# Earlier small loads and longer distances between VectorE pieces and the TensorE work that follows them, in a one-core DiT block

## The chip, the cores and the metric

The kernel runs on one core of a Trainium2 chip. Its metric is the device time in microseconds, the median of three runs. Five engines work beside each other, each through its own instructions in order: TensorE (PE, matmuls; PEld is its weight load), VectorE (DVE), ScalarE (ACT), GpSimd (POOL) and SyncE (SP), which here only issues DMAs. All of the large loads go out on SP.

## The reference

One block over 512 latent tokens and 256 context tokens of width 2048, in float32:

```python
mod   = silu(c) @ w_mod + b_mod            # 6 vectors of 2048; mod_c likewise from c_ctx
h_lat = rms_norm(x, nw[0]) * (1 + sc_m) + sh_m        # h_ctx likewise, with mod_c
p     = concat(h_ctx, h_lat) @ w_in
# lru: centred 4-tap conv of p's first 1024 columns, gates by 128x128 blocks, scans forward
#      and backward over context and latents; times gelu of the next 1024 columns
# gdn: conv + silu of q, k, v (8 heads of 128), l2-normalized q and k, beta and decay g from 32
#      gate columns, chunked delta rule forward and backward; rms_norm, times silu(z)
x = x + g_m * rms_norm(concat(lru, gdn)[latents] @ w_out, nw[1])
h = rms_norm(x, nw[2]) * (1 + sc_f) + sh_f
x = x + g_f * rms_norm(square(relu(h @ w_ff1)) @ w_ff2, nw[3])
```

The delta rule is, for each head and direction, a triangular solve within a chunk and a chain of state steps from chunk to chunk. Only the latents are returned.

## The kernel before

**Float32 by three products.** A weight piece is split into a rounded part `wh` (cast on ScalarE, L67) and a residue `wl` (subtraction on VectorE or GpSimd, L61), each with 3 buffers of 128x512, and each product of weights and activations is three matmuls: high by high, low by high, high by low. In the rows of the profile these are triples of lines: L338/341/342 (modulation), L524/525/526 (w_in), L1418/1419/1420 (w_out), L1467-1469, L1497-1499 and L1508-1510 (feed-forward).

**The stages.** (i) To about 135 us: c and c_ctx (16 rows of 128 each) and b_mod are loaded as rows of one page `pg`, turned into columns by a TensorE transpose against `ident` (function `columns`, L152; the copy behind it is L153), then `silc` = silu(c) and `csn`, its copy in matmul form (L171), are made on VectorE. 32 pieces of w_mod (tile `mr`, 1 MB each, 8 buffers; function `mload`, on SP) are split and multiplied. The context rows are normalized beside it. The small parameters (norm_w, the lru and gdn vectors) are loaded as rows of two more pages, `v2` and `v3`, and turned by `columns` behind the third piece (`if j == 2`). Two others, gdn_a_log and gdn_dt_bias, go into `alog`. (ii) To about 1085 us: the products with w_in, and beside them everything between the projections. (iii) To about 1480 us: the products with w_out (`project`, L1418-1420). (iv) The feed-forward to the end.

**Stage (ii) is the one that matters here.** `run_tiles` goes through a string of letters, `ORD`, one letter a column tile: k and l the gate columns of context and latents, c and g the q, k and v columns of the context's and the latents' heads, u and x the lru's input, y and z the two gates. A latent tile streams 512 columns, a context tile 256. A tile is four quads of 12 matmuls, the "streamed" matmuls; between quads the other work is put in. That work is a set of Python generators, and each `yield v, a, wait` ends a piece of it:

```python
                    if n == LAT or q % 2:
                        slot()
                        boundary()
```

`slot()` stands behind each quad of a latent tile and each second quad of a context tile. It gives a budget of 2.8 us of VectorE and 2.2 us of ScalarE (`RATE_V`, `RATE_A`) and lets tasks take their next piece while both budgets are positive; v and a are the piece's estimated costs in us, and `wait` is the number of slots that the task then sits out. All waits are written as multiples of H0, H1, H2 or H3, and all four are 1. Evacuations of tiles come first, then the tasks by priority. `boundary()` adds ordering edges, so that an instruction can't be moved more than 3 slots ahead on TensorE, SP and GpSimd, 2 on ScalarE and 1 on VectorE. So a piece that ends with a VectorE instruction and goes on with a TensorE one puts the TensorE instruction `wait` slots behind in TensorE's stream, and TensorE, which goes through its instructions in order, stops there if VectorE hasn't come that far.

**The pieces that the change touches.** In `gates` (L694, L715): the copy of the gate tile, its transposes, the softplus and the beta on VectorE (L693 among it), the cumulative sums on TensorE (L697 is the matmul that starts them). In `normed2` (L755): l2-normalized tokens on VectorE, then their transposes on TensorE (`transp`, L255). In `Group.evac` (L807): silu as tanh on ScalarE and a product on VectorE (helper line L64), then transposes (L255 again). In `Group.run`, for a group of heads (two context groups of four heads, four latent groups of two): the inversion of the triangular blocks, 31 elimination steps on VectorE (L927 is a transpose at their end), then copies of the blocks (L937-940), then products of pairs of 32x32 blocks on TensorE (L951) and of 64x64 blocks (L981/982), then state steps (L1024, L1038, L1048), then the outputs' rescaling (L1090) and their transposes (L255).

In `project`, a product over a pair of heads whose rows are not there yet runs `slot()` and `boundary()` until they are.

## Time and profile before

| | |
|---|---|
| median of 3 runs | 2808.57 us (2805.38 to 2812.1) |
| the profiled execution, its own time | 2803.51 us |
| its span | 2801.70 us |
| TensorE's granted clock, mean | 0.979 |
| TensorE, VectorE, ScalarE, GpSimd busy | 95, 60, 42, 21% of the span |
| bytes moved by DMA | 434.33 MB, mean 155 GB/s |

How to read it: "busy" leaves out waiting and the issuing of DMAs. In a row of groups or waits, the part before "<-" is what an instruction writes, behind it what it reads, with buffer numbers left out; in a row of waits the form is waiting instruction <- what it waited for, then total us, times, longest. In the timeline a row is start, duration, engine, line, operation, tiles, shapes and in brackets the wait just before it. "Granted clock" is the share of full speed that the chip's throttle gave TensorE. In the windows, each engine's busy time in a stretch stands with its count of instructions.

### The profile page before, as it was taken

The numbers are of one execution on the slowest core, as the hardware profiler recorded it, in microseconds if no ns is written. First come the engines' busy times: TensorE is split into PE (matmuls) and PEld (weight loads), VectorE is DVE, ScalarE is ACT, GpSimd is POOL, SyncE is SP. The second block draws the span as 40 slices with busy tenths as digits, with TensorE's granted clock in tenths as the row PEclk, the third lists the DMA queues.
The fourth block names the chain that finished last, engine by engine and source line by source line (L and its number), as shares of the span: only waits on it lengthen the run. The fifth ranks groups of instructions, "written<-read, shape, count | busy, mean of one in ns | idle before, by whom it ended". The sixth has DMA issues, their size and how long they took to land.

```text
span 2801.7 us, 39553 instructions
## 1 busy us (share of the span) xinstructions
PE 2654.4 (95%) x14253; PEld 2178.3 (78%) x14253; DVE 1682.8 (60%) x3287; ACT 1187.9 (42%) x2418; POOL 586.1 (21%) x552
## 2 busy tenths in 40 slices
PE   6989899899999998988999999999999999999998
PEld 2378797788777887776898887888888888888886
DVE  5786767777696777847598433444433444334436
ACT  4556576654556564535552222222222222222223
POOL 1155354344244354326310000000000000000002
PEclk9999999999999999989999999999999999999999
DMA  9664465566566667646778333333333333333335
GB/s 331 215 177 126 109 187 166 153 187 190 168 189 189 200 198 222 212 150 212 235 258 277 119 98 113 98 98 98 98 98 98 94 96 97 98 98 98 98 98 154
DMA packets 374968, 434.33 MB, mean 155 GB/s; under 512 B 22665, under 2 KB 212450, under 8 KB 374770
## 3 DMA queue, kind: packets, MB, share of 16 engines
q1 hardware_dynamic: 373984, 431.59, 49.6%
q8 instruction: 112, 1.84, 0.3%
q14 instruction: 86, 0.70, 0.1%
q10 hardware_dynamic: 786, 0.19, 0.0%
HBM read 401.31 MB, written 30.41 MB: 154 GB/s over the span
## 4 chain that ended last, share of the span: by engine, by line
PE 57%; DVE 4%; DMA 2%; POOL 1%; issue 1%; ACT 1%; SPq 0%; DVEq 0%; ACTq 0%; POOLq 0%
PE bk L1510 8%; PE bk L1508 8%; PE bk L1509 8%; PE bk L1497 7%; PE bk L1498 7%; PE bk L1499 7%; PE bk L1420 2%; PE bk L1419 2%; PE bk L1418 2%; PE bk L1469 1%; DVE pg L61 1%; PE bk L1468 1%; PE bk L1467 1%; DVE wl L61 1%; PE bk L524 1%
## 5 line engine op out<-in xcount | busy, mean ns | idle before, releaser
L67 ACT CAST wh<-wr 128x512 fp32r<-128x512 f32 x952 | 584.6, 618 | 1217.1 <-PE bk L1498 443.9
L61 DVE TENSOR_TENSOR wl<-wr,wh 128x512 fp32r<-128x512 f32 x642 | 464.1, 725 | 761.6 <-ACT wh L67 643.3
L61 POOL TENSOR_TENSOR wl<-wr,wh 128x512 fp32r<-128x512 f32 (+1 forms) x310 | 402.4, 1304 | 609.9 <-ACT wh L67 555.1
L1510 PE MATMUL bk<-wl,pg 128*128 128x512 f32 x960 | 373.6, 389 | 0.9 <-DVE wl L61 0.9
L1509 PE MATMUL bk<-wh,pg 128*128 128x512 f32 x960 | 373.5, 389 | 0.0
L1508 PE MATMUL bk<-wh,pg 128*128 128x512 f32 x960 | 373.5, 389 | 0.0
L1497 PE MATMUL bk<-H2h,wh 128*128 128x512 f32 x896 | 349.9, 390 | 0.0
L1499 PE MATMUL bk<-H2h,wl 128*128 128x512 f32 x896 | 349.0, 390 | 0.0
L1498 PE MATMUL bk<-H2l,wh 128*128 128x512 f32 x896 | 349.0, 390 | 0.0
L524 PE MATMUL bk<-Hlh,wh 128*128 128x512 f32 (+1 forms) x784 | 316.5, 404 | 0.0
L526 PE MATMUL bk<-Hlh,wl 128*128 128x512 f32 (+1 forms) x784 | 309.9, 395 | 1.8 <-POOL wl L61 1.8
L525 PE MATMUL bk<-Hll,wh 128*128 128x512 f32 (+1 forms) x784 | 310.1, 396 | 0.0
L61 POOL TENSOR_TENSOR big<-big,pg 128x512 f32<-128x512 f32 x9 | 12.0, 1340 | 1247.5 <-ACT pg L1570 1247.5
L1510 PEld LDWEIGHTS bk<-wl,pg 128*128 128x128 f32 x960 | 180.2, 188 | 38.8 <-DVE wl L61 1.3
L1508 PEld LDWEIGHTS bk<-wh,pg 128*128 128x128 f32 x960 | 180.2, 188 | 37.3
L1509 PEld LDWEIGHTS bk<-wh,pg 128*128 128x128 f32 x960 | 180.2, 188 | 37.2
L1498 PEld LDWEIGHTS bk<-H2l,wh 128*128 128x128 f32 x896 | 168.5, 188 | 35.4 <-issue 0.5
L1497 PEld LDWEIGHTS bk<-H2h,wh 128*128 128x128 f32 x896 | 168.6, 188 | 35.3 <-issue 0.2
L1499 PEld LDWEIGHTS bk<-H2h,wl 128*128 128x128 f32 x896 | 168.5, 188 | 35.2
L526 PEld LDWEIGHTS bk<-Hlh,wl 128*128 128x128 f32 (+1 forms) x784 | 148.4, 189 | 35.8 <-POOL wl L61 2.3
L524 PEld LDWEIGHTS bk<-Hlh,wh 128*128 128x128 f32 (+1 forms) x784 | 149.1, 190 | 30.9 <-ACT pg L1071 0.2
L525 PEld LDWEIGHTS bk<-Hll,wh 128*128 128x128 f32 (+1 forms) x784 | 148.8, 190 | 29.9
(346 smaller groups left out, 4514.5 us busy)
## 6 DMA issues: line engine op xcount, KB each, us to landing
wr<-in_w_ff SPq DMA_DIRECT2D x272, 512.0 KB
wr<-in_w_in SPq DMA_DIRECT2D x144, 512.0 KB
ld<-in_w_mod SPq DMA_DIRECT2D x256, 256.0 KB
mr<-in_w_mod SPq DMA_DIRECT2D x32, 1024.0 KB
wr<-in_w_out SPq DMA_DIRECT2D x64, 512.0 KB
pg<-vkD SPq DMA_DIRECT2D x88, 128.0 KB
ld<-in_x SPq DMA_DIRECT2D x32, 256.0 KB
vkD<-pg SPq DMA_DIRECT2D x24, 256.0 KB
```

The lines of the kernel that those rows point to most:

```text
L61: e.tensor_tensor(out=out, in0=a, in1=b, op=op)
L67: S.copy(hi, src)
L524: T.matmul(pt[:m, :n], wh, a, start=k == 0, stop=False)
L525: T.matmul(pt[:m, :n], wh, b, start=False, stop=False)
L526: T.matmul(pt[:m, :n], wl, a, start=False, stop=k == 15)
L1418: T.matmul(bk[t], mh[:, s_], h, start=st, stop=False)
L1497: T.matmul(bk[c], w[kk][0][:, s_], hh, start=k == 0, stop=False)
L1498: T.matmul(bk[c], w[kk][0][:, s_], hl_, start=False, stop=False)
L1499: T.matmul(bk[c], w[kk][1][:, s_], hh, start=False, stop=k == 15)
L1508: T.matmul(o, ah, h, start=k == 0, stop=False)
L1509: T.matmul(o, al, h, start=False, stop=False)
L1510: T.matmul(o, ah, l, start=False, stop=k == 3)
```

## The change

The loads of c, c_ctx and b_mod go from ScalarE's queue to SP's, ahead of all loads of w_mod. The ten other small loads are issued on ScalarE at once, ahead of everything else there; before, three of ScalarE's loads were those of c, c_ctx and b_mod, and eight of the ten stood behind the work on silu(c). The transposes that make columns of these parameters go from behind piece 2 of w_mod to behind piece 6. In stage (ii) seven waits change: 0 to 1 slot behind the gate tile's copy, 1 to 3 behind the softplus, 1 to 2 behind the l2-normalized tokens, the silu and the rescaled outputs, and a new wait of 1 slot between the copies of the inverted blocks and the pair products, with the costs given at the two places around it. No computation is added or removed.

```diff
--- before.py
+++ after.py
@@ -99,8 +99,8 @@
             return ap.rearrange("(r p) -> r p", p=P)
 
         v1 = page(shape=(P, P), tag="pg")
-        S.dma_start(v1[0:16], rows(A["c"][0]))
-        S.dma_start(v1[16:32], rows(A["c_ctx"]))
+        SP.dma_start(v1[0:16], rows(A["c"][0]))
+        SP.dma_start(v1[16:32], rows(A["c_ctx"]))
         wmod = A["w_mod"][0].rearrange("(k p) f -> p k f", p=P)
 
         def quad(nm_, dt=F32R):
@@ -116,23 +116,16 @@
                 mraw[j] = quad("mr", F32)
                 SP.dma_start(mraw[j], wmod[:, k:k + 4, col:col + 512])
 
-        S.dma_start(v1[32:128], rows(A["b_mod"][0]))
-        MB = 8
-        xraw = []
-        for j in range(MB):
-            mload(j)
-            if j in (1, 2):
-                xraw.append([page(tag="ld", bufs=ld_n) if 4 * (j - 1) + q < ld_n else page() for q in range(4)])
-                for q in range(4):
-                    SP.dma_start(xraw[-1][q], A["ctx"][0, (j - 1) * P:j * P, q * 512:(q + 1) * 512])
+        SP.dma_start(v1[32:128], rows(A["b_mod"][0]))
         c1 = const([P, P], F32, "c1")
         c2 = const([P, P], F32, "c2")
         c3 = const([P, 96], F32, "c3")
-
         alog = const([P, 32], F32, "alog")
         vs = []
 
         def small_loads():
+            S.dma_start(alog[:, 0:16], A["gdn_a_log"].rearrange("o d h -> o (d h)").to_broadcast([P, 16]))
+            S.dma_start(alog[:, 16:32], A["gdn_dt_bias"].rearrange("o d h -> o (d h)").to_broadcast([P, 16]))
             v2 = page(shape=(P, P), tag="pg")
             S.dma_start(v2[0:16], rows(A["norm_w"][0, 0]))
             S.dma_start(v2[16:32], rows(A["norm_w"][0, 2]))
@@ -143,10 +136,17 @@
             S.dma_start(v2[120:121], A["gdn_norm_w"])
             v3 = page(shape=(P, P), tag="pg")
             S.dma_start(v3[0:96], A["gdn_conv_w"][0].rearrange("j (r p) -> (j r) p", p=P))
-            S.dma_start(alog[:, 0:16], A["gdn_a_log"].rearrange("o d h -> o (d h)").to_broadcast([P, 16]))
-            S.dma_start(alog[:, 16:32], A["gdn_dt_bias"].rearrange("o d h -> o (d h)").to_broadcast([P, 16]))
             vs.extend([(v2, 121, c2), (v3, 96, c3)])
 
+        small_loads()
+        MB = 8
+        xraw = []
+        for j in range(MB):
+            mload(j)
+            if j in (1, 2):
+                xraw.append([page(tag="ld", bufs=ld_n) if 4 * (j - 1) + q < ld_n else page() for q in range(4)])
+                for q in range(4):
+                    SP.dma_start(xraw[-1][q], A["ctx"][0, (j - 1) * P:j * P, q * 512:(q + 1) * 512])
         def columns(src, n, dst):
             b = bank()
             T.transpose(b[:, :n], src[:n, :], ident[:n, :n])
@@ -166,7 +166,6 @@
         S.activation(sc_t, c1[:, 0:32], AF.Tanh, scale=0.5)
         stt(silc, sc_t, 1.0, c1[:, 0:32], ALU.add, ALU.mult)
         V.tensor_scalar_mul(silc, silc, 0.5)
-        small_loads()
         csn = const([P, 16, 2], F32, "csn")
         V.tensor_copy(csn, silc.rearrange("p (j k) -> p k j", j=2))
         cst = const([P, 16, 4], F32R, "cst")
@@ -342,7 +341,7 @@
                 T.matmul(pm[0][:4, :], cst[:, k, :], hl[i][1], start=False, stop=k == 14)
             del hl, h, l
             mload(j + MB)
-            if j == 2:
+            if j == 6:
                 while vs:
                     columns(*vs.pop(0))
             for g in list(late):
@@ -691,7 +690,7 @@
             def evac(pt):
                 gf = page()
                 V.tensor_copy(gf[:32, :n], pt[:32, :n])
-                yield 0.5, 0, 0
+                yield 0.5, 0, H0
                 b = bank()
                 for t in range(NT):
                     T.transpose(b[:, t * 32:(t + 1) * 32], gf[:32, t * P:(t + 1) * P], ident[:32, :32])
@@ -712,7 +711,7 @@
                 gl = const([P, W], F32R, "gl" + key)
                 V.tensor_copy(gh, g2)
                 tt(V, gl, g2, gh.bitcast(F32), ALU.subtract)
-                yield 3.1, 0.3, H0
+                yield 3.1, 0.3, 3 * H0
                 b = bank()
                 hw = W // 2
                 for i, (m, c0) in enumerate(((LE, 0), (GE, hw), (GT, 0), (LT, hw))):
@@ -752,7 +751,7 @@
                 tok = page()
                 tt(V, v4(tok), v4(b), r[:, 4 * i:4 * i + 4].unsqueeze(2).to_broadcast([P, 4, P]), ALU.mult)
                 toks.append(tok)
-            yield 1.3, 0, H0
+            yield 1.3, 0, 2 * H0
             for tok in toks:
                 b2 = transp(tok)
                 fm = page()
@@ -804,7 +803,7 @@
                     th = bank()
                     S.activation(th, cv, AF.Tanh, scale=0.5)
                     stt(cv, th, 1.0, cv, ALU.add, ALU.mult)
-                    yield 0.6, 0.5, H0
+                    yield 0.6, 0.5, 2 * H0
                     if kind == 2:
                         b = transp(cv)
                         v = page()
@@ -938,6 +937,7 @@
                         S.copy(blk(Ab[d], b, 32 * b, 32), Ud[d][32 * b:32 * b + 32])
                     for b in ((0, 1), (2, 3))[d]:
                         V.tensor_copy(blk(D64, b, 32 * (b % 2), 32), Dd[d][32 * b:32 * b + 32])
+                yield 0.8, 2.2, H1
                 bP = bank()[:, 0:256].rearrange("p (u i) -> p u i", i=32)
 
                 def pairs(d):
@@ -952,7 +952,7 @@
                                      start=True, stop=True)
                 Pn = page(shape=(P, 8, 32))
                 S.activation(Pn, bP, AF.Copy, scale=-1.0)
-                yield 0.8, 2.9, H1
+                yield 0, 0.7, H1
                 bU = [bank()[:, 0:256].rearrange("p (u i) -> p u i", i=32) for _ in range(2)]
                 for u in range(8):
                     for d in range(2):
@@ -1087,7 +1087,7 @@
                 yield 0.9, 2.4, 0
                 for p in range(2):
                     tt(V, v4(O[p]), v4(O[p]), r[:, 4 * p:4 * p + 4].unsqueeze(2).to_broadcast(sh4), ALU.mult)
-                yield 1.3, 0, H0
+                yield 1.3, 0, 2 * H0
                 while any(h0 + p not in szs for p in range(2)):
                     yield 0, 0, H0
                 sz = []
```

In the rows below, taken from each engine's instructions in order, a row is line, operation, written tile <- read tiles, shape. Lines 168 to 940 of the changed file are one lower than before; from 951 on they are the same.

ScalarE at the program's start, before (`pg_88` is the page of c, c_ctx and b_mod; the CAST rows begin the first piece of w_mod):

```order
L102 DMA pg_88<-in_c 16x128
L103 DMA pg_88<-in_c_ctx 16x128
L119 DMA pg_88<-in_b_mod 96x128
L146 DMA alog<-in_gdn_a_log 128x16
L147 DMA alog<-in_gdn_dt_bias 128x16
L374 ACT_TABLE_LOAD
L374 ACTIVATE nea<-alog 128x16
L67 CAST wh_234<-mr_92 128x512
```

and of the change (`pg_98` and `pg_106` are the pages v2 and v3; one more load, into `alog` from L127, stands ahead of the first row):

```order
L128 DMA alog<-in_gdn_dt_bias 128x16
L130 DMA pg_98<-in_norm_w 16x128
L131 DMA pg_98<-in_norm_w 16x128
L132 DMA pg_98<-in_lru_conv_b 8x128
L133 DMA pg_98<-in_lru_conv_w 32x128
L134 DMA pg_98<-in_lru_gate_b 32x128
L135 DMA pg_98<-in_lru_lambda 16x128
L136 DMA pg_98<-in_gdn_norm_w 1x128
L138 DMA pg_106<-in_gdn_conv_w 96x128
L373 ACT_TABLE_LOAD
L373 ACTIVATE nea<-alog 128x16
L67 CAST wh_234<-mr_108 128x512
```

The three loads of c, c_ctx and b_mod have left ScalarE, and eight loads that stood behind later casts now stand ahead of the first cast.

TensorE in stage (ii), where the third latent group's pair products (L951) begin, before (`Hlh`, `Hll` are the latents' normalized rows, `A` the group's blocks):

```order
L524 MATMUL bk_11447<-Hlh_1136,wh_11404 128x512
L525 MATMUL bk_11447<-Hll_1137,wh_11404 128x512
L526 MATMUL bk_11447<-Hlh_1136,wl_11405 128x512
L524 MATMUL bk_11447<-Hlh_1136,wh_11404 128x512
L525 MATMUL bk_11447<-Hll_1137,wh_11404 128x512
L526 MATMUL bk_11447<-Hlh_1136,wl_11405 128x512
L951 MATMUL bk_11484<-pg_11444,A_9369 32x32 x2
L524 MATMUL bk_11447<-Hlh_1136,wh_11404 128x512
L525 MATMUL bk_11447<-Hll_1137,wh_11404 128x512
L526 MATMUL bk_11447<-Hlh_1136,wl_11405 128x512
```

and of the change (`M` are the rows that w_out multiplies):

```order
L525 MATMUL bk_11386<-Hlh_1140,wl_11400 128x512
L523 MATMUL bk_11386<-Hlh_1140,wh_11399 128x512
L524 MATMUL bk_11386<-Hll_1141,wh_11399 128x512
L525 MATMUL bk_11386<-Hlh_1140,wl_11400 128x512
L1418 MATMUL bk_11545<-wh_11430,M_11535 128x512
L1418 MATMUL bk_11546<-wh_11430,M_11535 128x512
L951 MATMUL bk_11607<-pg_11492,A_9907 32x32 x2
L951 MATMUL bk_11607<-pg_11491,A_9908 32x32
L1419 MATMUL bk_11545<-wh_11430,M_11535 128x512
L1420 MATMUL bk_11545<-wl_11431,M_11535 128x512
```

The first pair products have gone from between the last streamed products with w_in to among the first with w_out, 29 streamed matmuls further on.

TensorE in stage (iii), where the fourth latent group's first state step stands (L1024, `S` is the state), before:

```order
L1418 MATMUL bk_12675<-wh_12866,M_11682 128x512
L1419 MATMUL bk_12675<-wh_12866,M_11682 128x512
L1420 MATMUL bk_12675<-wl_12867,M_11682 128x512
L1024 MATMUL bk_12910<-S_1192,pg_10823 128x128
L1024 MATMUL bk_12910<-S_1192,pg_10830 128x128
L1024 MATMUL bk_12910<-S_1192,pg_10823 128x128
L1024 MATMUL bk_12910<-S_1192,pg_10830 128x128
L1418 MATMUL bk_12674<-wh_12878,M_11682 128x512
L1419 MATMUL bk_12674<-wh_12878,M_11682 128x512
L1420 MATMUL bk_12674<-wl_12879,M_11682 128x512
```

and of the change:

```order
L1418 MATMUL bk_12613<-wh_12869,M_11537 128x512
L1419 MATMUL bk_12613<-wh_12869,M_11537 128x512
L1420 MATMUL bk_12613<-wl_12870,M_11537 128x512
L1418 MATMUL bk_12614<-wh_12869,M_11537 128x512
L1419 MATMUL bk_12614<-wh_12869,M_11537 128x512
L1420 MATMUL bk_12614<-wl_12870,M_11537 128x512
L1024 MATMUL bk_12938<-S_1192,pg_10779 128x128
L1024 MATMUL bk_12938<-S_1192,pg_10786 128x128
L1024 MATMUL bk_12938<-S_1192,pg_10779 128x128
L1024 MATMUL bk_12938<-S_1192,pg_10786 128x128
L1038 MATMUL bk_12956<-pg_12937,A_11584 128x128
```

The state step has gone from between products with w_out to behind the last of them in this stretch, 12 streamed matmuls further on, so that the next step's products (L1038) follow it with none between. From there on both kernels have the same order.

## The prediction

> **What bounds the kernel now.** I read the page first (busy shares, chain), then the waits of TensorE, then the windows of the stretches in which they fall, then the timeline of the first 40 us and of the last waits.
>
> ```profile
> PE 2654.4 (95%) x14253; PEld 2178.3 (78%) x14253; DVE 1682.8 (60%) x3287; ACT 1187.9 (42%) x2418; POOL 586.1 (21%) x552
> PE 57%; DVE 4%; DMA 2%; POOL 1%; issue 1%; ACT 1%; SPq 0%; DVEq 0%; ACTq 0%; POOLq 0%
> ```
>
> TensorE (PE) is busy 95% of the span and most of the chain that ended last. It is idle for 2801.7 - 2654.4 = 147 us. The change removes no matmul, so what it can win lies in these 147 us, and in matmuls that run slowly after a wait. Who is waited for:
>
> ```profile
> PE bk L255 <- DVE pg L64: 19.8, 7, 5.7
> PE bk L951 <- DVE pg L927: 11.8, 4, 9.2
> PE bk L255 <- DVE pg L61: 10.5, 3, 7.3
> PE bk L152 <- DMA pg<-in_b_mod: 8.2, 1, 8.2
> PE bk L697 <- DVE pg L693: 6.2, 2, 3.4
> PE bk L338 <- DVE csn L171: 6.0, 1, 6.0
> PE bk L152 <- DMA pg<-in_gdn_conv_w: 5.3, 1, 5.3
> ```
>
> The columns are total us, times, longest. Three rows belong to the start (19.5 us), four to transposes and small products that follow a VectorE (DVE) piece (48.3 us). By stretches:
>
> ```profile
> core 0: us, PE busy (x) PEld busy (x) DVE busy (x) ACT busy (x) POOL busy (x), PEclk, DMA share, GB/s
> 20.00:135.00 115.00, 103.64 (x402) 34.99 (x400) 82.58 (x183) 65.63 (x130) 14.27 (x13) 0.93 0.79 274
> 136.00:224.00 88.00, 72.70 (x568) 69.74 (x567) 75.10 (x163) 47.38 (x106) 47.97 (x39) 0.96 0.56 159
> 455.00:575.00 120.00, 101.51 (x626) 82.92 (x625) 95.25 (x209) 68.74 (x159) 44.86 (x38) 0.93 0.51 151
> 930.00:1030.00 100.00, 99.68 (x522) 84.61 (x521) 78.16 (x160) 58.79 (x139) 42.47 (x43) 1.00 0.63 190
> 1030.00:1081.00 51.00, 41.77 (x191) 34.35 (x189) 45.21 (x104) 22.07 (x34) 23.55 (x19) 0.94 0.71 223
> 1199.00:1240.00 41.00, 27.70 (x201) 25.80 (x199) 22.67 (x74) 12.33 (x47) 3.22 (x5) 0.86 0.51 157
> 1240.00:2802.00 1562.00, 1531.13 (x7080) 1275.53 (x7080) 775.77 (x1257) 498.45 (x880) 105.91 (x82) 0.99 0.41 129
> ```
>
> Where TensorE waits, VectorE is nearly full (75.1 of 88 us, 45.2 of 51). That limits what a larger distance can win. After 1240 us the order of work is the same in both kernels, so the change is decided before that.
>
> **The change part by part.** *The start.* The rows of the first 35 us:
>
> ```profile
> 3.36 0.46 ACTq L147 DMA_DIRECT2D alog<-in_gdn_dt_bias  x1
> 8.23 0.45 PE L152 MATMUL bk<-ident,pg 128*128 128x128 f32 x1 [8.23 <-DMA pg<-in_b_mod]
> 10.70 0.22 ACT L374 ACTIVATE nea<-alog 128x16 f32<-128x16 f32 x1 [5.57 <-DMA alog<-in_gdn_a_log]
> 10.82 1.64 ACT L67 CAST wh<-mr 128x512 fp32r<-128x512 f32 x3
> 13.40 0.28 DVE L153 COPY c<-bk 128x128 f32<-128x128 f32 x1
> 14.65 1.87 PE L338 MATMUL bk<-mr,csn 128*2 128x512 f32 x2 [5.98 <-DVE csn L171]
> 29.59 0.43 PE L152 MATMUL bk<-ident,pg 121*128 121x121 f32 x1 [5.32 <-DMA pg<-in_gdn_conv_w]
> 104.70 5.29 SPq L487 DMA_DIRECT2D wr<-in_w_in  x3
> 133.21 0.38 PE L312 MATMUL bk<-sel,pg 4*128 4x2 f32 x2 [0.86 <-DVE pg L306]
> ```
>
> ScalarE's (ACT) first cast stands behind the log-decay load, until 10.82; VectorE copies c only behind the casts of the first piece, though the transpose was over at 8.7; csn follows, and the first weight matmul starts at 14.65. In the new order c, c_ctx and b_mod go out first on SP, so the transpose comes earlier, but VectorE still has two residues of the first piece ahead of the copy. ScalarE issues ten loads ahead of its first cast; at about 0.46 us each they take about 5 us, the last six of them also wait for an earlier landing, and the first piece of weights is three issues (1.4 us) later. I take the first cast at 9 us and the first weight matmul at 12.5: 2 won. The wait of 5.3 at 29.6 goes altogether, because the two small transposes move from the third piece to the seventh, when their loads are long there; part of it returns as a wait for the fourth piece of weights. I take 4 of 5.3. From then on TensorE sets the pace (103.6 busy of 115): the first load behind the 32 pieces is issued at 104.70, while TensorE ends with them after 133. So 6 won at the start arrive at the end of the stage. Bounds: 0 (the weights' arrival is the limit) and 6.0 + 5.3 = 11.
>
> *Distances.* A slot is 12 matmuls of 512 columns, 0.23 us apart in the rows below, so one slot more gives VectorE 2.8 us. The transposes behind silu (L807) get one more: 7 waits, at most 7 x 2.8 = 19.6, less the 5.7 - 2.8 = 2.9 that the longest keeps: up to 17. Tokens and outputs (L755, L1090): of 10.5 us in 3 waits the 7.3 lie behind the last streamed matmul, where no distance helps: up to 3. The gates (L694, L715): 24 matmuls of 512 columns, or 30 of 256, now lie between: up to 6. The inversion's pair products (L940): the third latent group's move back by 30 to 40 matmuls, 7 to 9 us against the wait of 9.2, and the three smaller waits go: up to 11, but VectorE itself is full there (45.2 of 51), so I count 8. Together 34.
>
> *The clock.* A wait costs twice:
>
> ```profile
> 1180.14 1.47 PE L255 MATMUL bk<-ident,pg 128*128 128x128 f32 x8 [1.40 <-DVE pg L61]
> 1182.26 0.63 PE L1418 MATMUL bk<-wh,M 128*128 128x512 f32 x1
> 1182.69 0.63 PE L1419 MATMUL bk<-wh,M 128*128 128x512 f32 x1
> 1185.11 0.39 PE L1419 MATMUL bk<-wh,M 128*128 128x512 f32 x1
> 1185.34 0.40 PE L1420 MATMUL bk<-wl,M 128*128 128x512 f32 x1
> 1181.00:1184.50 3.50, 3.50 (x90) 2.56 (x90) 3.50 (x5) 0.62 (x1) 0.83 (x1) 0.51 0.64 214
> 1184.50:1188.00 3.50, 3.50 (x59) 2.66 (x49) 1.29 (x3) 2.41 (x6) 0.86 (x1) 1.00 0.26 85
> ```
>
> After a wait of only 1.40 us the granted clock is 0.51 for 3.5 us and matmuls start 0.43 apart, then 0.23: 3.5 x 0.47 = 1.6 us more. Of the 16 waits above in the four rows I take 8 as long enough to bring this, and gone: 13 us at most. A rule of the Trainium skill would make that less: "TensorE: Matmul & The Clock Gate" ("Why this matters for your kernels") has the clock fall only after one idle window of about 3.4 us. By that rule only the few waits above 3.4 would pay, some 3 x 1.6 = 5 instead of 13, and the sum below would be 4 smaller; the row of 1.40 us speaks against it.
>
> *What these 34 + 13 = 47 come to.* The waited-for engine runs in order and keeps all its work. A transpose put later lets TensorE go on, but TensorE then comes earlier to the next thing that VectorE owes. Bounds: 0 (the waits only move) and 47. Between them I go by the windows: in 455:575 TensorE has 120 - 101.5 = 18.5 idle; at the 0.89 share (45.2 / 51) that VectorE reaches where it is fullest, its 95.25 us need 107, so 13 of 18.5 can go; in 136:224 its 75.1 need 84, so 4 of 15.3; in 1030:1081 nothing but what is moved out. That is 17 of 43, about 0.4, and a little better where VectorE has more room. I take 0.45 of 47: 21.
>
> *The tail.* The last group's first state step now stands behind the last streamed matmul, not 12 ahead of it:
>
> ```profile
> 1198.42 1.05 PE L1024 MATMUL bk<-S,pg 128*128 128x128 f32 x8
> 1202.05 1.05 PE L1038 MATMUL bk<-pg,A 128*128 128x128 f32 x8
> 1205.80 1.06 PE L1024 MATMUL bk<-S,pg 128*128 128x128 f32 x8
> ```
>
> Nothing covers it any more: 1202.05 - 1198.42 = 3.6 us, of which I count 3 as lost. Bounds: 0 and one whole step, 1205.80 - 1198.42 = 7.4.
>
> The sum: 6 + 21 - 3 = 24 won. The profiled execution took 2803.51 us (span 2801.7), so 2779.5; the median of the runs shown, 2808.57, lies 5 above it, which gives **2784.6**.
>
> **Rivals.** *A, the waits only move.* VectorE, full in the windows above, is the limit and the distances win nothing; the start wins 6, the tail loses 3: 2808.6 - 3 = 2805.6. For it: 45.2 of 51. Against it: VectorE is busy 60% of the span, and 78 of 100 just ahead.
>
> *B, all of it.* 11 + 47 - 0 = 58 won: 2750.6. Against it: the longest silu wait keeps 2.9 by the distance alone, and 136:224 has room for 4.
>
> *C, slower: VectorE's work bunches ahead of the third latent group.* With longer distances the second latent group's pair products stand 288 streamed matmuls later than before (2940 instead of 2652 into the stream), so its inversion and its state steps run between 900 and 1081 us. VectorE has 100 - 78.2 + 51 - 45.2 = 28 us free there. It decides once more than these 28 are added: an inversion with its state steps and rescaling, put at 45, would leave TensorE waiting for 17, with 1.6 us of slow clock in each of 5 waits, and groups three and four fall back by as much, into the uncovered tail: 17 + 8 + 3 lost, with only the 6 of the start won and the other gains used up by VectorE: + 22, 2830. Against it: other pieces stand earlier in exchange, and VectorE's total is unchanged.
>
> *D, the start does not do what it says.* The ten issues on ScalarE wait for landings as long as the one above (from 3.36 to 10.70 at most, 7.3); the first cast comes at 13 to 14, not 9, and the start loses 3 instead of winning 6: 21 - 3 - 3 = 15 won, 2793.6.
>
> **How the numbers follow.** The forecast has 0.50 with its own range of 2770 to 2800 (distances at 0.2 to 0.75 of 47); A 0.17, B 0.08, C 0.13, D 0.12. The range for 8 in 10 reaches from 2765, which cuts off B alone, to 2810, which takes in A and D and leaves C out. A measurement of this kernel tells about 0.2% (5.6 us) from no change: faster means below 2803, slower above 2814. Faster: 0.50 + 0.08 + 0.12 + 0.04 of A = 0.74; same: 0.12 of A and 0.01 of C; slower: the rest of C and 0.01 of A, 0.13.
>
> **What would show it.** Start: no wait on gdn_conv_w, the first weight matmul near 12.5 instead of 14.65, the first load of w_in still near 105 or before and the end of the mod stage near 127. Distances: the row L255 <- DVE L64 (one line earlier in the new file) near 4 to 8 instead of 19.8, the gates' row gone, the 9.2 at the third inversion 3 or less, and fewer slices with a granted clock below 1. VectorE's windows fuller. Tail: the last state step group ends 3 later than its last streamed matmul does now. I am wrong if the sum of TensorE's waits stays near 147 with other names (A), if a wait above 10 stands between 900 and 1100 us (C), or if the weights' first cast comes after 12 (D).

## The result: 2789.5 us, and where the profile after differs

The changed kernel took 2789.51 us (median of 6 runs, 2782.82 to 2792.65) against 2804.53 for the kernel before (6 runs beside and ahead of it): a ratio of 0.9941, 95% interval 0.9922 to 0.996. That is 15 us by the medians and 16.5 (11 to 22) by the ratio; forecast were 24. Its profiled execution took 2792.65 us with a span of 2790.9, and is the slowest of the six, so the two profiles are only 10.8 us apart. Four executions beside the experiments, three of the kernel before and one of another, took 3006 to 14929 us against the usual 2800 and are left out of the ratios and medians.

The page of the changed kernel, busy times and chain, and its longest waits of TensorE (total us, times, longest):

```profile
PE 2661.4 (95%) x14253; PEld 2181.3 (78%) x14253; DVE 1676.4 (60%) x3287; ACT 1183.7 (42%) x2418; POOL 585.0 (21%) x552
PE 69%; DVE 8%; issue 3%; DMA 2%; ACT 2%; POOL 1%; SPq 0%; DVEq 0%; ACTq 0%; POOLq 0%
PE bk L525 <- POOL wl L61: 15.6, 19, 2.5
PE bk L523 <- ACT wh L67: 12.2, 9, 3.3
PE bk L254 <- DVE pg L64: 8.2, 5, 2.8
PE bk L254 <- DVE pg L61: 8.0, 2, 7.3
PE bk L1418 <- ACT M L67: 6.8, 2, 6.4
PE bk L152 <- DMA pg<-in_b_mod: 5.7, 1, 5.7
PE bk L337 <- DMA ld<-in_ctx: 5.6, 1, 5.6
```

The rows that the change was to shorten are shorter: the transposes behind silu waited 19.8 us and wait 8.2, the 9.2 at the third inversion and the gates' row have left the list, and so has the wait on gdn_conv_w. At the top now stand two rows that were small before. In the kernel before, the same two waits of the streamed w_in products for their own weights read

```profile
PE bk L526 <- POOL wl L61: 8.8, 9, 1.8
PE bk L524 <- ACT wh L67: 4.2, 6, 1.3
```

so 13.0 us have become 27.8. The wait for `M`, the rows that w_out multiplies, has gone from 0.4 to 6.8.

The start, from the timeline of the changed kernel:

```profile
5.66 0.45 PE L152 MATMUL bk<-ident,pg 128*128 128x128 f32 x1 [5.66 <-DMA pg<-in_b_mod]
6.33 0.32 ACTq L138 DMA_DIRECT2D pg<-in_gdn_conv_w  x1
8.38 1.66 ACT L67 CAST wh<-mr 128x512 fp32r<-128x512 f32 x3 [0.19 <-DMA mr<-in_w_mod]
10.24 0.28 DVE L153 COPY c<-bk 128x128 f32<-128x128 f32 x1
11.71 1.87 PE L337 MATMUL bk<-mr,csn 128*2 128x512 f32 x2 [5.60 <-DMA ld<-in_ctx]
97.65 7.01 SPq L486 DMA_DIRECT2D wr<-in_w_in  x3
```

The ten issues on ScalarE are over at 6.65, the first cast starts at 8.38 (before: 10.82) and the first weight matmul at 11.71 (14.65). The first load of w_in goes out at 97.65 instead of 104.70, so 7 us reach the end of the stage.

How the lead over the kernel before goes on is read from the start of the n-th streamed matmul (w_in and w_out counted through, from the timeline):

| n | before | changed | lead |
|---|---|---|---|
| 0 | 135.9 | 128.8 | 7.1 |
| 864 | 296.2 | 294.9 | 1.3 |
| 1728 | 510.0 | 490.9 | 19.1 |
| 3072 | 946.7 | 914.7 | 32.1 |
| 3552 | 1093.9 | 1066.5 | 27.4 |
| 3744 | 1169.2 | 1152.9 | 16.3 |
| 3839, last ahead of the tail | 1201.8 | 1187.2 | 14.6 |
| 3840, first behind it | 1240.0 | 1230.0 | 10.0 |

Two thirds of the largest lead are lost again, but part of it had only been put off: between the streamed matmuls TensorE also does the other work, and up to n = 3072 it has done 1874 of these other matmuls in the kernel before and 1726 in the changed one. The 148 take some 12.6 us, an estimate from the durations in the two traces. At n = 3744 it is 2490 and 2466, some 3 us, so most of what was put off has been made up by then. The windows of the stretch from 3526 to 3744 and of the tail, of the kernel before:

```profile
1081.80:1169.20 87.40, 86.39 (x671) 72.62 (x670) 64.79 (x181) 46.09 (x100) 33.89 (x32) 0.98 0.74 231
1201.80:1240.00 38.20, 24.90 (x186) 23.42 (x184) 20.94 (x69) 11.65 (x45) 2.77 (x4) 0.85 0.48 148
```

and of the changed one:

```profile
1053.20:1152.90 99.70, 91.05 (x659) 76.07 (x658) 68.51 (x177) 48.15 (x109) 39.82 (x42) 0.90 0.72 227
1187.20:1230.00 42.80, 29.72 (x195) 27.49 (x194) 22.07 (x73) 11.65 (x45) 2.79 (x4) 0.82 0.43 131
```

Columns as in the prediction (length, PE, PEld, DVE, ACT and POOL busy, granted clock, DMA share, GB/s). The stretch has nearly the same work in both kernels (452 and 440 other matmuls). In the changed one it has 8.7 us of idle TensorE instead of 1.0 and a granted clock of 0.90 instead of 0.98, which costs 10.0 us of full-speed work instead of 1.7 (the two overlap where TensorE idles at half clock). The tail is 4.6 longer.

**Why the weights are late** stands in the timeline of the changed kernel near 501 us:

```profile
500.41 0.74 DVE L64 SCALAR_TENSOR_TENSOR pg<-bk,c,pg 128x511 f32<-128x511 f32 x1
501.24 0.60 ACT L804 ACTIVATE bk<-pg 128x512 f32<-128x512 f32 x1 [7.32 <-DVE pg L64]
501.78 1.64 ACT L67 CAST wh<-wr 128x512 fp32r<-128x512 f32 x3
502.44 0.50 PE L523 MATMUL bk<-Hlh,wh 128*128 128x512 f32 x1 [3.26 <-ACT wh L67]
502.46 3.76 POOL L61 TENSOR_TENSOR wl<-wr,wh 128x512 fp32r<-128x512 f32 x3 [5.14 <-ACT wh L67]
503.79 0.50 PE L525 MATMUL bk<-Hlh,wl 128*128 128x512 f32 x1 [0.62 <-POOL wl L61]
```

ScalarE stood 7.32 us at the silu's tanh (L804), which waits for the conv's taps on VectorE. Three casts of weights stood behind it and then ran without a further wait; GpSimd waited for the casts, and TensorE for both. Most of what VectorE does between 491 and 501 us are elimination steps of an inversion, and the taps stand among them, so they come late. Between 136 and 1240 us ScalarE waited at the tanh for VectorE, before and in the changed kernel:

```profile
ACT bk L805 <- DVE pg L64: 65.0, 23, 6.9
```

```profile
ACT bk L804 <- DVE pg L64: 67.1, 20, 8.9
```

With the table loads that stand ahead of some of these tanhs and wait for VectorE too, and the shorter rows of this line, it is 94.5 and 108.3. So the wait was nearly as long before. What is new is that TensorE, held less by VectorE, comes to the casts behind it: of its waits for weights in this stage, those that end within 6 us behind such a wait of over 1 us are 6.4 us before and 18.1 us with the change (within 4 us 6.4 and 14.3, within 9 us 9.9 and 22.4). What the rest of them, 10.3 and 13.8 us, hang on isn't followed here.

### The profile page after: what moved, and what is told of

It reads as the page before. It is cut to its first block, busy times and chain, and to the rows that moved or that the text cites. A ratio compares the mean times of both kernels' runs of the same rounds, so it can differ in the third digit from the quotient of the medians.

```text
span 2790.9 us, 39585 instructions
## 1 busy us (share of the span) xinstructions
PE 2661.4 (95%) x14253; PEld 2181.3 (78%) x14253; DVE 1676.4 (60%) x3287; ACT 1183.7 (42%) x2418; POOL 585.0 (21%) x552
## 4 chain that ended last, share of the span: by engine, by line
PE 69%; DVE 8%; issue 3%; DMA 2%; ACT 2%; POOL 1%; SPq 0%; DVEq 0%; ACTq 0%; POOLq 0%
PE bk L1510 8%; PE bk L1509 8%; PE bk L1508 8%; PE bk L1498 7%; PE bk L1499 7%; PE bk L1497 7%; PE bk L523 3%; PE bk L525 3%; PE bk L524 3%; PE bk L1419 2%; PE bk L1420 2%; PE bk L1418 2%; DVE pg L64 2%; DVE bk L64 1%; DVE pg L61 1%
## 5 line engine op out<-in xcount | busy, mean ns | idle before, releaser
L523 PEld LDWEIGHTS bk<-Hlh,wh 128*128 128x128 f32 (+1 forms) x784 | 148.7, 190 | 36.6 <-ACT wh L67 6.6
```

The source lines that it names most:

```text
L523: T.matmul(pt[:m, :n], wh, a, start=k == 0, stop=False)
```

## Experiments: the two halves of the change

**The start alone** (all loads and the moved transposes; the seven waits as before).

> Only the start of the change: the loads and the transposes behind the seventh piece, with all waits as before. Theory (the start's gain arrives whole, because TensorE sets the pace of the first stage): first streamed w_in matmul at 128 to 130 us instead of 136, time 6 to 8 us below the kernel before. Rival (the earlier end of the first stage is taken back by VectorE, which is fuller there): first streamed matmul as early, but 0 to 3 us below before.

Measured: 2795.86 us against 2802.04, ratio 0.9976 (0.9964 to 0.9987): 6.7 us less (3.6 to 10). The first streamed matmul stands at 130.2, and the lead, 5.8 there, is still 5.6 at n = 3744. The start's gain arrives whole.

**The distances alone** (the seven waits; the start as before).

> Only the longer distances, with the start as before. Theory (part of the waits moves to the streamed matmuls, which wait for their own weights): TensorE's waits for VectorE shorter by about 30 us, the streamed matmuls' waits on wh and wl longer by about 14, and 8 to 10 us below before. Rival A (the waits only move): within 3 us of before. The prediction's own term: 21 - 3 = 18 below.

Measured: 2796.22, ratio 0.9974 (0.9961 to 0.9988): 7.3 less (3.4 to 11). This is the theory's size, and under half of the 18 that the prediction has for it. The two halves add up: 6.7 + 7.3 = 14.0 against 16.5 for both.

## Experiments: which distance brings it

**The silu's distance alone**, on the kernel before:

```diff
-                    yield 0.6, 0.5, H0
+                    yield 0.6, 0.5, 2 * H0
```

> Only the silu's distance (1 slot to 2 ahead of its transposes). If the distances' gain is mostly here, as the wait of 19.8 us in 7 places says: 5 to 9 us below before. If the gain needs all distances together, or the waits only move: within 3 us.

Measured: 2824.34, ratio 1.0079 (1.0061 to 1.0097): 22 us **slower**. Neither reading had that. Its own row did what it should, the rows of others did not:

```profile
PE bk L951 <- DVE pg L927: 8.3, 2, 7.8
PE bk L255 <- DVE pg L64: 6.1, 3, 5.0
PE bk L578 <- DVE rqy L64: 4.5, 1, 4.5
PE bk L1419 <- POOL M L61: 4.5, 1, 4.5
PE bk L719 <- DVE pg L61: 3.2, 1, 3.2
```

The silu's transposes wait 6.1 us instead of 19.8, but groups start a slot later, and pieces that nobody touched now meet VectorE unready: the first context group's pair products wait 7.8 us, the lru's gates 4.5, the cumulative sums 3.2.

**All but the silu's distance** (the changed kernel with this one back at one slot).

> The changed kernel with the silu's distance back at one slot, all else of the change kept. Silu's distance alone had cost 22 us. If it costs as much beside the others, 2765 to 2772 (about 20 below the changed kernel at 2788). If the distances only work together (the transposes behind the silu were the largest row of waits, 19.8 us, and would stand in the way again): 5 to 12 above the changed kernel, 2793 to 2800.

Measured: 2788.43, ratio to before 0.9951 (0.9937 to 0.9965), the changed kernel's own ratio being 0.9941. Neither reading had that. Beside the others the silu's distance is worth nothing: the transposes behind silu wait 13.4 instead of 8.2, and the time is the same. The prediction had half of its 34 us of waits there.

**All but the slot ahead of the pair products.**

> The changed kernel without the new slot ahead of the pair products. The prediction's term (8 of the 34 us of waits, times 0.45): 3 to 6 above the changed kernel, with a wait of 6 to 10 us again at the third inversion. Rival (the wait there has only changed its name, now 6.4 us for the first rows of w_out): within 3 us of the changed kernel.

Measured: 2795.83, ratio 0.9977 (0.9966 to 0.9988), 6 to 10 above the changed kernel (by the medians and by the ratios). The pair products wait again, 6.18 us at 537 and 6.05 at 1051 us, the second of them at the third latent group, as the prediction's term says; it is worth some two to three times what the sum had for it (8 x 0.45 = 3.6).

**Silu and pair slot together**, on the kernel before.

> The kernel before with two distances only, the silu's and the new slot ahead of the pair products. Theory (silu's distance alone loses 22 because groups start later and TensorE then meets the first context group's pair products 7.8 us before VectorE is done with the inversion, and falls to a slow clock more often): with the slot there the loss is gone, 3 to 8 below before, 2795 to 2800. Rival (the loss lies in other places of the schedule): still 10 or more above before, 2812 or more.

Measured: 2804.9, ratio 1.0000 (0.9988 to 1.0013), in neither range. The new slot takes back the whole 22 us, but the two together win nothing. Nor is it shown that the loss hung on the pair products' own wait: that is 12.8 us before, 9.2 with the silu's distance alone and 1.1 with both. By the starts of the streamed matmuls, half of the loss lies ahead of the 3072nd (820.3 us from the first to there instead of 810.8, and 824.3 with both, which has then done 80 more of the other matmuls than the kernel before). The other half lies among the products with w_out: from the 3526th to the 3744th it takes 87.4 us before, 97.3 with the silu's distance alone and 85.4 with both. That part is what the slot takes back.

**The outputs' distance back at one slot**, in the changed kernel:

```diff
-                yield 1.3, 0, 2 * H0
+                yield 1.3, 0, H0
                 while any(h0 + p not in szs for p in range(2)):
```

> The changed kernel with the distance of tokens and outputs as before at the outputs (one slot ahead of the transposes of the rescaled outputs), so that the last group's tail stands as before. The prediction counted 3 us as lost there: 2 to 4 below the changed kernel. Rival (the tail's length is VectorE's and ScalarE's chain of state steps, which starts no earlier): within 2 us.

Measured: 2789.32, ratio 0.9953 (0.9938 to 0.9967), by the medians as fast as the changed kernel, by the ratios 3 slower. The tail is 42.0 us in this profile, as long as with the change (42.8), so it isn't this edit that lengthens it. The rival's size is right; what the tail's length follows is told further down.

## Experiments: ScalarE at the tanh

**A slot between the taps and the tanh**, in the changed kernel, for the last tile of each pair:

```diff
-                    yield 1.7, 0.6, 0
+                    yield 1.7, 0.6, H0 if i == len(self.hp[p]) - 1 else 0
                     if i < len(self.hp[p]) - 1:
                         return
                     th = bank()
                     S.activation(th, cv, AF.Tanh, scale=0.5)
```

> The changed kernel with one more slot between the conv's taps on VectorE and the silu's tanh on ScalarE. Theory (ScalarE waits some 70 us for those taps with weight casts queued behind, and this is where the distances' gain is given back): ScalarE's waits of the tanh for VectorE fall from 67 to under 30 us, the streamed matmuls' waits on wh and wl from 30 to about 18, and the time falls by 5 to 10 us below the changed kernel (20 to 26 below before). Rival (VectorE is the limit, and what is taken from one wait comes back in another): within 3 us of the changed kernel, 13 to 19 below before.

Measured: 2772.22, ratio to before 0.9894 (0.9872 to 0.9916): 30 less, and 13 (by the ratios) to 17 (by the medians) below the changed kernel, which is more than the theory had. The waits of the tanh and of the streamed products for the casts, in this kernel:

```profile
ACT bk L804 <- DVE pg L64: 14.9, 9, 3.6
PE bk L523 <- ACT wh L67: 9.8, 3, 5.1
```

**The same slot on the kernel before, alone.**

> The kernel before with one change alone: one more slot between the conv's taps on VectorE and the silu's tanh on ScalarE. If ScalarE's waiting ahead of weight casts costs by itself: 10 to 15 below before, with ScalarE's waits of the tanh for VectorE under 30 us instead of 65. If it only shows once TensorE is no longer held by VectorE itself: within 4 us of before; if a single distance bunches work as the silu's did: 10 or more above.

Measured: 2785.64 (2780.16 to 2795.62), ratio 0.9945 (0.9925 to 0.9964): 15 less from one line, as much as the whole change. The tanh waits 22.4 instead of 65.0 (51.6 instead of 94.5 with the table loads). But here the waits for weights did not fall (21.3 instead of 16.6 us); those of the transposes did, which the slot moves back as well (58.3 to 38.6), and so did the cost of the half clock (38.0 to 26.9, as in the table below). So the first reading has the size, but its reason, the casts behind the tanh, isn't what the trace shows here.

```profile
ACT bk L805 <- DVE pg L64: 22.4, 14, 5.6
```

**The same distance for the transposes without moving the tanh** (3 slots behind the silu's product in the changed kernel).

> The changed kernel with the silu's transposes one slot further back (3 instead of 2), the tanh where it was: the transposes then stand as far behind as in the run with the slot ahead of the tanh, but ScalarE meets the tanh as early as before. Theory (ScalarE, held by the tanh ahead of the weight casts, gave the gain back): within 4 us of the changed kernel, 2784 to 2793, and the tanh still waits over 60 us. Rival (what helped there was the transposes' distance): as fast as that run, 2768 to 2776.

Measured: 2776.29, ratio 0.9901 (0.9883 to 0.9918). By the time alone the rival is right, to 0.3 us. By the trace the two kernels win at different places:

```profile
ACT bk L804 <- DVE pg L64: 58.4, 18, 13.6
PE bk L523 <- ACT wh L67: 13.1, 11, 2.9
PE bk L525 <- POOL wl L61: 11.7, 19, 0.9
```

With 3 slots ScalarE still waits 58.4 us and the streamed products 27.4 for their weights, 13.3 of them within 6 us behind a wait at the tanh of over 1 us; with the slot ahead of the tanh no wait for weights stands there. The 3744th streamed matmul starts at 1150.5, 2.4 ahead of the changed kernel, and 10 us come from a shorter tail (1183.2 to 1216.0, 32.8 instead of 42.8), in which 152 instead of 192 matmuls are left. With the slot ahead of the tanh that matmul starts at 1136.8, 16 ahead, and the tail is as long as it was (42.0). So the tanh does hold the weights, as the theory has it; but it isn't the only way to those 13 us.

**Two slots ahead of the tanh.**

> The kernel with the slot ahead of the tanh, with two slots in its place. Theory (what is left of the tanh's wait, 15 us, still holds casts): the tanh waits under 5 us, 0 to 5 us less than with one slot, 2767 to 2772. Rival (groups start later by a slot more, and bunch): 5 or more above it, 2777 or more.

Measured: **2748.13**, ratio 0.9791 (0.9771 to 0.9811): 59 us less than before (55 by the medians), 24 below one slot by the medians. It beats both kernels. The reason given is not the one: the tanh waits 14.0 us, as with one slot. What fell is the sum of TensorE's waits and its time at half clock, below. Of the 24 us, 17 lie between the 1728th and the 3072nd streamed matmul (418.3 us with one slot, 401.2 with two): TensorE's waits there fall from 16.4 to 3.7 us and the cost of the half clock from 6.8 to nothing. Why the second slot does that is not shown.

```profile
PE bk L254 <- DVE pg L61: 12.3, 3, 7.3
PE bk L523 <- ACT wh L67: 4.8, 3, 3.4
PE bk L525 <- POOL wl L61: 2.9, 6, 0.6
ACT bk L804 <- DVE pg L64: 14.0, 8, 4.0
455.00:575.00 120.00, 118.30 (x782) 97.97 (x782) 104.20 (x227) 81.93 (x188) 55.70 (x56) 1.00 0.62 191
```

The last row is a window of the prediction, though as the order has moved it doesn't hold quite the same work: TensorE was idle there for 18.5 of 120 us, and is for 1.7. VectorE does 104.2 us of work in it instead of 95.25, a share of 0.87.

## Experiment: what a wait costs beside itself

The clock's records lie on a fixed grid of 3.41 us. Grid units of the kernel before, each pair a unit and the next:

```profile
904.50:907.90 3.40, 1.55 (x10) 1.03 (x9) 3.37 (x5) 0.37 (x1) 2.44 (x3) 1.00 0.11 43
907.90:911.30 3.40, 3.40 (x10) 2.64 (x9) 3.36 (x7) 0.34 (x1) 2.25 (x2) 0.51 0.70 195
1177.70:1181.10 3.40, 1.63 (x9) 0.96 (x9) 3.37 (x6) 2.50 (x5) 2.03 (x2) 0.99 0.34 85
1181.10:1184.50 3.40, 3.40 (x89) 2.46 (x89) 3.40 (x5) 0.62 (x1) 0.73 (x1) 0.50 0.65 219
```

The wait of 1.40 us that the prediction quotes was not alone in its unit: TensorE was busy for 1.63 of 3.40 us. Over the profiles of ten kernels (all of this document but the last four to be run: silu and pair slot together, silu at 3, two slots, the filling; the first 380 units of each behind its first clock record, at 15 to 21 us), of units at full clock with TensorE idle for over 60%, all 110 were followed by one at half clock; of those idle for 50 to 60%, 36 of 47; for 40 to 50%, 9 of 69; for less, 45 of 3258. Of these 45, 36 lie in the first 137 us, where the products with w_mod run (36 of 283 units there, 9 of 2975 later); what sets that stage apart isn't shown. At half clock a unit with 20% idle or more was followed by another in 68 of 70 cases. So a wait mostly costs half of the next unit, 1.7 us, if it fills over half of a unit with its neighbours (always at over 60%), and less often if it falls across a border.

To make that an experiment, TensorE is kept busy in the 7.28 us in which it waits for the last group's rescaled outputs: 48 matmuls of constants into the bank that the transposes then overwrite, in the kernel with one slot ahead of the tanh. The call for the last group's first output becomes `transp(O[p], 48 if h0 == 6 and p == 0 else 0)`.

```diff
-        def transp(src):
+        def transp(src, fill=0):
             b = bank()
+            for _ in range(fill):
+                T.matmul(b[:, :P], ones, ident, start=True, stop=True)
```

> The kernel with the slot ahead of the tanh, and in it 48 matmuls of 128x128 constants in the place where TensorE waits 7.28 us for the last group's rescaled outputs (their results are overwritten; nothing else moves). Theory (a wait costs twice, since the granted clock falls behind a unit of 3.4 us in which TensorE is mostly idle): granted clock 1.00 instead of 0.5 in the 7 us behind that place, the streamed matmuls there 0.23 us apart instead of 0.43, and 2 to 4 us less than without, near 2769. Rival (the clock there follows something else): the clock stays low, same time.

Measured: 2772.19, ratio to before 0.988 (0.9862 to 0.9898); without the filling 2772.22. The timeline without it:

```profile
1207.37 1.97 PE L254 MATMUL bk<-ident,pg 128*128 128x128 f32 x8 [7.28 <-DVE pg L61]
1211.60 0.63 PE L1418 MATMUL bk<-wh,M 128*128 128x512 f32 x1
1212.02 0.63 PE L1419 MATMUL bk<-wh,M 128*128 128x512 f32 x1
```

and with it (the lines stand two lower in the file):

```profile
1197.23 10.88 PE L254 MATMUL bk<-ident,ones 128*128 128x128 f32 x96
1207.95 1.04 PE L256 MATMUL bk<-ident,pg 128*128 128x128 f32 x8
1211.46 0.39 PE L1422 MATMUL bk<-wl,M 128*128 128x512 f32 x1
1211.69 0.40 PE L1420 MATMUL bk<-wh,M 128*128 128x512 f32 x1
```

The clock did what the theory says: the transposes take 1.04 instead of 1.97, the streamed matmuls stand 0.23 apart instead of 0.43, and from the first of them to the twelfth it takes 3.0 instead of 5.1 us. That wins 3. But each of the 48 shows as two records, so that they last 10.88 us, 3.3 longer than the wait, and take it back. A filling of half the length was not run.

## Why the prediction was right, and where its sum was not

One table serves for all of it. The stage from the first streamed matmul to the first one behind the tail, in each profile, is split into TensorE's waits by kind (sums of the rows of the waits view), half of the time at half clock, and the rest (idle time at half clock is counted in both, so the rest is somewhat too small):

| kernel | stage | transposes, pairs | weights | other waits | half-clock cost | rest |
|---|---|---|---|---|---|---|
| before | 1104.1 | 58.3 | 16.6 | 16.3 | 38.0 | 974.9 |
| changed | 1101.2 | 24.6 | 31.8 | 22.1 | 41.9 | 980.8 |
| distances alone | 1096.2 | 24.3 | 33.1 | 21.4 | 36.1 | 981.3 |
| silu alone | 1120.0 | 35.2 | 23.4 | 40.1 | 46.0 | 975.3 |
| slot at the tanh, alone | 1082.0 | 38.6 | 21.3 | 19.1 | 26.9 | 976.1 |
| changed + slot | 1081.5 | 35.4 | 13.6 | 23.7 | 33.5 | 975.3 |
| changed, silu at 3 | 1085.4 | 18.9 | 27.4 | 24.1 | 32.4 | 982.6 |
| changed + 2 slots | 1056.8 | 30.5 | 11.7 | 16.6 | 26.3 | 971.7 |

The rest is the same within some 11 us while the stage varies by 63 (975 to 984 in the profiles not listed, that with the filling left aside): what a schedule changes here is mostly waits and clock. What makes the rest 6 us larger in the changed kernel than before isn't traced to a row.

*The start* (6 forecast): 6.7 measured, and by its mechanism. The cast came at 8.38 (forecast 9), the matmul at 11.71 (12.5), the wait on gdn_conv_w is gone. Rival D is out: the landings that the issues waited for did not delay the cast.

*The waits named* (34 forecast to go): 58.3 - 24.6 = 33.7 went, and 30.3 (48.3 to 18.0) by the four rows alone that the prediction counts. This term was right in sum, and wrong in its parts, since the silu's half of it loses 22 us by itself and is worth nothing beside the others, and the pair slot's part is worth 6 to 10.

*How much of them remains won* (0.45 of 47, so 21): this is the step that was too large. The distances brought 7.3 with the tail in it. Of the 33.7 us, 15.2 came back as waits for weights and 5.8 as others, the rows of w_out above all. The factor was drawn from VectorE's full windows; the largest part of what came back is ScalarE standing in order at a tanh, with some 8 to 12 of the 15.2 us of waits for weights behind it. The prediction asked which VectorE piece TensorE meets next and not who else waits for VectorE with TensorE's work behind it. That the waits for weights fell from 31.8 to 13.6 us when the tanh was put a slot later, with none left behind a wait at the tanh, shows the place. That the time then falls by this wait is only partly shown: other waits took most of the 18 us, and nearly half of what arrived came through the clock. The time stayed inside the forecast's own range, 2770 to 2800, all the same, which owes something to luck: that range is 30 us wide around a gain of 24, and the distances brought 7.3 instead of 18.

*The clock* (13 of the 47): did not come. The half-clock cost is 38.0 before, 41.9 in the changed profile and 36.1 with the distances alone. The prediction read one row of 1.40 us as if a wait of that size did it by itself, when its unit was idle for 1.77 of 3.40 us, and took as gone what the new waits bring again. The rule of the Trainium skill that it was set against ("TensorE: Matmul & The Clock Gate", "Why this matters for your kernels") would have made the gain 4 smaller and the time 2788.6, nearer to the measured one. The same page of the Trainium skill ("What's actually happening") has a free-running window of 3413 ns, with which the grid here agrees; that one whole window must be idle does not hold here, where over half of one is mostly enough (36 of 47 and 110 of 110 cases).

*The tail* (3 lost): 38.2 to 42.8, 4.6 lost in this profile, in the place named: 192 matmuls instead of 184 are left behind the last streamed one, and the 8 are the state step. It isn't a fixed price. The tail follows how much of the last group is left for it: 30.2 us with 128 matmuls (without the silu's distance), 30.6 to 35.9 with 152 (without the pair slot, with the tanh's slot alone, with the silu's at 3, with silu and pair slot), 36.6 to 39.9 with 184 and 38.7 to 42.8 with 192.

*The rivals.* A, that the waits only move, is out for the whole change and half right for the distances. C, slower by bunching, did not come in the changed kernel. Its size is what the silu's distance does alone, 22 slower, but not its mechanism, VectorE filling between 900 and 1081: that kernel is 3 us faster than before from the 3072nd to the 3526th streamed matmul (961 to 1093 us), and loses ahead of it and among the products with w_out.

*What was to be seen.* The row of L64 at 8.2 (forecast 4 to 8, so just above), the gates' row down to 1.0 (L697, which is the transposes of the gate tile; the cumulative sums are L719), the pair wait gone, the first load of w_in earlier, the first stage's last product at 127.7 (forecast 127): right. TensorE's idle time is 129.5 us instead of 147, much of it under other names. Fewer slices below full clock: wrong, three of the page's 40 stand at 8 tenths instead of one. VectorE's windows fuller: wrong in three of the prediction's four (72.2 instead of 75.1, 94.0 instead of 95.25, 39.7 instead of 45.2; 81.5 instead of 78.2).

## What to carry to other kernels

When an engine's wait is made shorter by moving it back, look for a second engine that waits in order for the same late work and has the first one's input queued behind that wait; look at what each engine has queued there, and try that wait too. Here moving it back by one slot was worth as much as this whole change, both alone and on top of it, but the waits for weights fell only on top of it; a second slot won 24 us more, and why isn't shown. Distances of a hand-written order can't be judged one by one: one alone lost 22 us, with one other distance beside it nothing. And when leads are compared, count what each kernel has put off: of a lead of 32 us, some 12.6 were work still to be done. Count idle time by its sum within the clock's fixed units of 3.41 us, not by single waits.

## What the runs showed of the hardware

Unexpected was how sharp the clock's rule is: behind a unit of 3.41 us with TensorE idle for over 60%, the next was at half clock in 110 of 110 cases, and below 40% in 45 of 3258, only 9 of them behind the first 137 us, wherever the single waits lay. And the loss isn't the same for the same order of work. The kernels with and without the filling have one order on every engine up to it, and their windows ahead of it, without and with, are

```profile
1025.00:1095.00 70.00, 57.57 (x435) 45.88 (x434) 39.03 (x68) 38.15 (x77) 31.53 (x36) 0.83 0.63 198
```

```profile
1025.00:1095.00 70.00, 57.20 (x459) 44.89 (x458) 42.52 (x79) 38.83 (x81) 29.75 (x34) 0.90 0.65 205
```

TensorE is idle for 12.4 and 12.8 us in them, and the granted clock is 0.83 and 0.90: 12 and 7 us lost. The windows don't hold quite the same work; from the 3526th to the 3744th streamed matmul it is the same (408 other matmuls), and there, with waits of 7.9 and 8.0 us, the half clock costs 10.2 and 3.6, and the stretch takes 98.8 and 94.4. Once the clock is low, idle shares that cost nothing at full clock keep it low: behind a unit with 20 to 40% idle the next was at half clock in 4 of 266 cases at full clock, and in 24 of 26 at half clock.
